# Large GpSimd instructions written as two halves each, and the new tokens' scores as plain fp32 matmuls, in a two-layer decoder step

## The chip, the core and the metric

The kernel runs on one NeuronCore of a Trainium2 chip. The metric is the device time of one execution in microseconds (us). The engines are called by the profile's names: PE (TensorE matmuls), PEld (its weight loads), DVE (VectorE), ACT (ScalarE), POOL (GpSimd) and SP (SyncE, which issues the DMAs). Each engine works through its own list of instructions in order.

## The reference, cut to what matters

Two layers run over 1024 prompt tokens and, in the same pass, over 64 new tokens: 8 sequences of 8 tokens, each with its own cache of old keys and values. Each layer projects every token to nine parts, and runs a gated branch and an attention branch with three dilation groups of 8 heads.

```python
u, v, z_a, q, k, val, z_b, g_a, g_b = split_projection(jnp.dot(h, w_in))
vn = layer_norm(jax.nn.gelu(v), gm_ln_g, gm_ln_b)
y_a = jax.nn.gelu(u) * gm_spatial(vn) * jax.nn.silu(z_a)      # gated branch
...
# new tokens, group g (window win, dilation dil: (128,1), (512,4), (2048,16)):
k_all = jnp.concatenate([buf[:, :, 0], k[:, :, g]], axis=1)   # cached keys, then the new ones
kg = jnp.take(k_all, idx, axis=1)
s = jnp.einsum('bthd,btjhd->bhtj', q, kg) * (HEAD_DIM ** -0.5)
p = jnp.exp(s - logsumexp(s)); o = jnp.einsum('bhtj,btjhd->bthd', p, vg)
```

## The kernel before, in words

All matrices are fp32. For the projections each operand is split in two fp32r parts, a high part (an ACT copy, L243) and the rest (a subtraction, L249, or L247 where POOL and DVE take half each); a product is then three matmuls, hi·hi, hi·lo and lo·hi (L741; L1382 behind the attention). `split` does this for weights (`whi`, `wlo`, 128x1024, subtraction on POOL) and for activations and cached rows (`chl`, `vhl`, `pt`, 128x512 or less, subtraction on DVE).

A layer is 80 jobs of one weight tile each (val, q and k; z_b, g_a, v, g_b, z_a, u). A job is three pieces, one for each token block (384, 384 and 320 columns): `piece` issues 24 matmuls on PE. Three times in a piece it calls `tick`, which moves the work beside the projections: the prompt's attention, the cached scores and values, and a queue of generators that each go on to their next `yield` when their turn comes. So the order of work on every engine is that in which the program writes it; what a `yield` more or less does is put the next instructions some eight matmuls of PE later or earlier. `pause(n)` is n yields; `idle(n)` first runs the urgent generators, then n yields.

Beside the projections run:

- `cache_step`, the cached keys and values of the two dilated groups: POOL multiplies a loaded key tile by the queries (L377, L381, tiles `kq`), DVE adds up (L386); POOL multiplies a value tile by the probabilities (L430, tiles `vq`), DVE adds up (L415, L416).
- `sample`, the rest of the new tokens: four k units (`weights(rg)`, two sequences each) and four v units (`outputs(rg)`). In a k unit, each sequence's queries are copied by ACT in six pieces into a zeroed tile `qb`, DVE subtracts the copies for the low part (L1218), and PE multiplies them by the 128 cached keys of group 0 (L1228, keys split as `chl`) and by the new keys (L1236); DVE puts both halves together in `rows` (L1242). L1264 ff. are the softmax. In a v unit, L1315 and L1316 multiply probabilities by split values (`chl`).
- `gmlp`, the gated branch: for each block of 128 tokens `stats` (transposes on PE, L1099; statistics on DVE), the block before's `spatial` (plain fp32 matmuls, L1132), two yields, then `normalise` (DVE, L1113). `ev_u` of the first u job needs all of it: `drain` goes on turning the generators until `gm_done`.
- `ada`, the modulation of the next layer (L602, L579), the rest of which is drained at the end of layer 0.

The prompt's attention uses `kz` (zeroed key tiles written by ACT, L240) and L870 for its scores.

Of the kernel before, what the change touches and what calls it, by code (L numbers as in the profile page):

```python
# [24 lines left out]
FT = mybir.dt.float32  # L25
# [7 lines left out]
NB = 8  # L33
# [146 lines left out]
class Builder:  # L180
# [166 lines left out]
    def scores(self, l, g, pr):  # L347
# [57 lines left out]
    def values(self, l, rg, pv):  # L405
# [101 lines left out]
    def setup(self):  # L507
# [28 lines left out]
        self.s_d = [[d([8, NB, NT, 128], f"sd{l}{g}") for g in (1, 2)] for l in range(L)]  # L536
        self.vn_d = [d([3, SMP, 512], f"vnd{l}") for l in range(L)]
# [517 lines left out]
    def gmlp(self, l):  # L1055
# [84 lines left out]
        for n in (8, 0, 1, 2, 3, 4, 5, 6, 7):  # L1140
# [3 lines left out]
            yield from self.pause(2)  # L1144
# [27 lines left out]
    def sample(self, l):  # L1172
        nc, a, ident = self.nc, self.a, self.pk("ident")
        whole = self.apool.tile([128, 6144], FR, name=self.nm("qb"), tag="act")
        big = whole[:, 0:768]
        pt = whole[:, 768:1536].rearrange("p (a b) -> p a b", b=128)
        qs, kn = [whole[:, o:o + 768].bitcast(FT).rearrange("p (a b) -> p a b", b=SMP) for o in (1536, 2304)]
        vw = whole[0:24, 3072:4096].rearrange("p (a b) -> p a b", a=2)
        sel2 = whole[:, 4096:4160]
        knh = whole[:, 4160:4352].rearrange("p (a b c) -> p a b c", a=2, b=12)  # L1180
        for t, d in ((qs, self.qs_d[l]), (kn, self.kn_d[l])):
            self.load(t, d.rearrange("c p t -> p c t"))
        t = self.half(name="sel2")[:, 0:64]
        self.load(t, a["pack"][:, NPACK:NPACK + 64])
        nc.gpsimd.memset(whole[:, 0:768].bitcast(FT), 0.0)
        nc.vector.memset(whole[:, 768:1536].bitcast(FT), 0.0)
        pstep = list(big.ap[0])[0]

        def diag(off, ap, h2):
            v = big[64 * h2:64 * h2 + 64]  # L1190
            return bass.AP(tensor=v.tensor, offset=v.offset + off, ap=[[pstep, 64]] + ap)
# [3 lines left out]
        for x, rg in units:  # L1195
            for b in (2 * rg, 2 * rg + 1):
                if x == "v":
                    seq += [a["vc1"][l, b, i] for i in range(2)]
                seq.append(a[x + "c0"][l, b])
# [6 lines left out]
        yield from self.idle(2)  # L1206
        pn = {}

        def weights(rg):
            rows = self.slot([128, 1024], name="rows")[:, 0:408]  # L1210
            for b2 in range(2):
                b = 2 * rg + b2
                cols = slice(8 * b, 8 * b + 8)
                for h2 in range(2):
                    for o, ap, src in self.q_places(qs, slice(64 * h2, 64 * h2 + 64), cols, h2):
                        hi, lo = diag(o, ap, h2), diag(o + 32, ap, h2)
                        self.copy(hi, src)
                        nc.vector.tensor_tensor(lo, src, hi.bitcast(FT), op=OP.subtract)  # L1218
                self.split(knh[:, 0], knh[:, 1], kn[:, :, cols])
                yield from self.idle(2)  # L1220
                s = [self.ps("s") for _ in range(2)]
                hi, lo = next(st)
                for kt in range(4):
                    first, last = kt % 2 == 0, kt % 2 == 1
                    c = slice(kt * 128, kt * 128 + 128)
                    mm = [(64, hi), (32, lo)]
                    for m, t in (mm[::-1] if last else mm):
                        nc.tensor.matmul(s[kt // 2][0:m, 0:128], big[:, kt * 64:kt * 64 + m], t[:, c],  # L1228
                                         start=first and m == 64, stop=last and m == 64)
                yield  # L1230
                for g in range(3):
                    for kt in range(4):
                        base = g * 256 + kt * 64
                        mm = [(64, 0), (32, 1)]
                        for m, e in (mm[::-1] if kt % 2 else mm):
                            nc.tensor.matmul(s[kt // 2][0:m, 128 + 8 * g:136 + 8 * g], big[:, base:base + m],  # L1236
                                             knh[:, e, g * 4 + kt, :], start=kt % 2 == 0 and m == 64,
                                             stop=kt % 2 == 1 and m == 64)
                for qd in range(2):
                    t = self.half(name="slo")[0:32, 0:152]  # L1240
                    self.copy(t, s[qd][32:64, 0:152])
                    nc.vector.tensor_tensor(rows[64 * b2 + 32 * qd:64 * b2 + 32 * qd + 32, 128:280], s[qd][0:32, 0:152], t,  # L1242
                                            op=OP.add)
                yield
# [465 lines left out]
```

## Time and profile before

| | |
|---|---|
| median of 3 runs | 3123.28 us (3117.01 to 3130.36) |
| the profiled execution | 3131.33 us, of which the span is 3129.5 us |
| PE busy | 3010.8 us |
| DVE, ACT, POOL busy | 1687.0, 1231.3, 1357.9 us |

The span runs from the first instruction to the last; what lies around it is 1.8 us. The profiled execution is 8 us longer than the median.

### The profile page before, as it was taken

The numbers are of one execution on the slowest core, as the hardware profiler recorded it, in microseconds if no ns is written. First come the engines' busy times: TensorE is split into PE (matmuls) and PEld (weight loads), VectorE is DVE, ScalarE is ACT, GpSimd is POOL, SyncE is SP. The second block draws the span as 40 slices with busy tenths as digits, with TensorE's granted clock in tenths as the row PEclk, the third lists the DMA queues.
The fourth block names the chain that finished last, engine by engine and source line by source line (L and its number), as shares of the span: only waits on it lengthen the run. The fifth ranks groups of instructions, "written<-read, shape, count | busy, mean of one in ns | idle before, by whom it ended". The sixth has DMA issues, their size and how long they took to land.

```text
span 3129.5 us, 51144 instructions
## 1 busy us (share of the span) xinstructions
PE 3010.8 (96%) x19136; PEld 2865.4 (92%) x19136; DVE 1687.0 (54%) x3583; ACT 1231.3 (39%) x3089; POOL 1357.9 (43%) x959
## 2 busy tenths in 40 slices
PE   6999999999998999999999999999999999999998
PEld 4999899999988998879989999999999889989998
DVE  7445546462265756466773545454513657553666
ACT  5454444444233133343444444444432331322432
POOL 4666556462143322123446755656612432222333
PEclk8999999999999999999999999999999999999999
DMA  6335353444353335466644364435343542434665
GB/s 223 113 103 119 98 101 120 95 121 84 112 180 113 122 108 167 157 236 227 211 153 134 86 142 81 119 106 114 106 81 119 171 130 95 138 102 149 223 211 172
DMA packets 262288, 425.92 MB, mean 136 GB/s; under 512 B 116140, under 2 KB 169144, under 8 KB 262040
## 3 DMA queue, kind: packets, MB, share of 16 engines
q1 hardware_dynamic: 262040, 422.65, 45.4%
q8 instruction: 151, 2.47, 0.3%
q14 instruction: 97, 0.79, 0.1%
HBM read 349.96 MB, written 72.61 MB: 135 GB/s over the span
## 4 chain that ended last, share of the span: by engine, by line
PE 82%; DVE 8%; DMA 4%; issue 3%; ACT 2%; POOL 1%; SPq 0%; DVEq 0%; ACTq 0%; POOLq 0%
PE pspj L741 53%; PE pspj L1382 14%; PE pss L870 4%; PE pso L916 3%; PE pspt L895 2%; PE psmi L602 1%; DMA kq<-in_kc_dram 1%; DVE qb L1218 1%; DMA craw<-in_wada_dram 1%; DVE chl L249 1%; PE psmi L998 1%; DMA wraw<-in_win_dram 1%; ACT whi L243 1%; PE pss L1236 1%; PE pspt L1132 1%
## 5 line engine op out<-in xcount | busy, mean ns | idle before, releaser
L741 PE MATMUL pspj<-act,whi 128*128 128x384 f32 (+1 forms) x7680 | 1967.0, 339 | 6.5 <-DVE act L674 3.5
L741 PEld LDWEIGHTS pspj<-act,whi 128*128 128x128 f32 x7680 | 1352.7, 190 | 42.4 <-issue 7.4
L741 PE MATMUL pspj<-act,wlo 128*128 128x384 f32 (+1 forms) x3840 | 1264.3, 329 | 2.3 <-POOL wlo L247 2.3
L249 POOL TENSOR_TENSOR wlo<-wraw,whi 128x1024 fp32r<-128x1024 f32 x154 | 371.4, 2411 | 970.5 <-ACT whi L243 766.5
L741 PEld LDWEIGHTS pspj<-act,wlo 128*128 128x128 f32 x3840 | 729.0, 190 | 3.4 <-POOL wlo L247 3.4
L1382 PE MATMUL pspj<-act,whi 128*128 128x384 f32 (+1 forms) x1536 | 373.4, 326 | 0.5 <-ACT act L243 0.4
L243 ACT ACTIVATE whi<-wraw 128x1024 fp32r<-128x1024 f32 x280 | 293.9, 1051 | 112.0 <-DMA wraw<-in_wgm_dram 48.1
L247 POOL TENSOR_TENSOR wlo<-wraw,whi 128x512 fp32r<-128x512 f32 x126 | 192.3, 1531 | 328.4 <-ACT whi L243 268.7
L882 ACT ACTIVATE ssb<-ssb,ast 128x128 f32<-128x128 f32 (+1 forms) x384 | 170.2, 444 | 394.2 <-DVE ast L878 394.1
L878 DVE CUSTOM_DVE_ANT_0 ssb<-pss,pack 128x128 f32<-128x128 f32 (+1 forms) x384 | 119.4, 348 | 318.1 <-PE pss L870 316.5
L1382 PEld LDWEIGHTS pspj<-act,whi 128*128 128x128 f32 x1536 | 270.0, 188 | 1.0 <-ACT act L243 0.7
L1382 PE MATMUL pspj<-act,wlo 128*128 128x384 f32 (+1 forms) x768 | 250.2, 326 | 0.0
L1010 ACT ACTIVATE th<-pspj 128x384 f32<-128x384 f32 x168 | 79.2, 471 | 428.6 <-PE pspj L741 396.5
L787 POOL TENSOR_TENSOR r<-r,sin 128x384 f32<-128x384 f32 x144 | 139.0, 965 | 141.4 <-DVE r L786 121.4
L249 DVE TENSOR_TENSOR chl<-craw,chl 128x512 fp32r<-128x512 f32 x182 | 147.2, 840 | 86.7 <-ACT chl L243 86.2
L377 POOL TENSOR_TENSOR kq<-kq,qb 128x1024 f32<-128x1024 f32 x64 | 153.5, 2404 | 63.1 <-DMA kq<-in_kc_dram 45.9
L381 POOL TENSOR_TENSOR kq<-kq,qb 128x512 f32<-128x512 f32 x128 | 167.6, 1314 | 19.8 <-DMA kq<-in_kc_dram 9.2
L386 DVE TENSOR_REDUCE sc<-kq 128x16 f32<-128x1024 f32 x128 | 155.7, 1216 | 21.2 <-POOL kq L377 20.7
L870 PE MATMUL pss<-kz,q 128*128 128x256 f32 x560 | 155.4, 385 | 10.6 <-ACT kz L240 10.6
L430 POOL TENSOR_TENSOR vq<-vq,pv 128x1024 f32<-128x1024 f32 x64 | 132.3, 2081 | 50.0 <-DMA vq<-in_vc_dram 20.6
L1382 PEld LDWEIGHTS pspj<-act,wlo 128*128 128x128 f32 x768 | 144.2, 188 | 0.0
L247 DVE TENSOR_TENSOR wlo<-wraw,whi 128x512 fp32r<-128x512 f32 x126 | 109.3, 868 | 40.0 <-ACT whi L243 36.5
(211 smaller groups left out, 3676.2 us busy)
## 6 DMA issues: line engine op xcount, KB each, us to landing
wraw<-in_win_dram SPq DMA_DIRECT2D x160, 512.0 KB
kq<-in_kc_dram SPq DMA_DIRECT2D x64, 512.0 KB
vq<-in_vc_dram SPq DMA_DIRECT2D x64, 512.0 KB
craw<-in_wada_dram SPq DMA_DIRECT2D x48, 512.0 KB
wraw<-in_wgm_dram SPq DMA_DIRECT2D x48, 512.0 KB
wraw<-in_wo_dram SPq DMA_DIRECT2D x48, 512.0 KB
kq<-in_kc_dram SPq DMA_DIRECT2D x64, 256.0 KB
craw<-in_vc_dram SPq DMA_DIRECT2D x32, 512.0 KB
```

The costliest lines, as they stand in the source:

```text
L243: self.nc.scalar.activation(hi, src, AF.Copy)
L247: e.tensor_tensor(lo[:, c], src[:, c], hi[:, c].bitcast(FT), op=OP.subtract)
L249: (eng or self.nc.vector).tensor_tensor(lo, src, hi.bitcast(FT), op=OP.subtract)
L377: nc.gpsimd.tensor_tensor(v, v, x, op=OP.mult)
L381: nc.gpsimd.tensor_tensor(v[:, f], v[:, 1], x[f], op=OP.mult)
L386: nc.vector.tensor_reduce(sc[:, :, i].rearrange("p h j -> p j h"), ts.pop(i)[0].rearrange("p a (j h d) -> p (a j) h d", h=2, d=64), axis=A ...
L430: nc.gpsimd.tensor_tensor(v, v, p.unsqueeze(3).to_broadcast([128, 2, 8, 64]), op=OP.mult)
L741: nc.tensor.matmul(ps[:, :w], a[:, k, :], h[:, b, k, :w], start=(n == 0), stop=(n == 23))
L787: nc.gpsimd.tensor_tensor(t2, t2, self.sin[:, s], op=OP.mult)
L870: nc.tensor.matmul(s[:, 256 * j:256 * j + 256], u["q"][:, 128 * b:128 * b + 128], self.kz[:, (b - n + j) % 4].rearrange("p h c -> p (h c)" ...
L882: nc.scalar.activation(x[:, h, :w], x[:, h, :w], AF.Exp, bias=st[:, h * 8 + b:h * 8 + b + 1], scale=-1.0, accum_out=st[:, 16 + h * 8 + b:1 ...
L1382: self.nc.tensor.matmul(ps[:, :w], ws[a][:, k, :], hs[b][k][:, :w], start=(n == 0), stop=(n == 3 * nk - 1))
```

## The change

GpSimd's subtractions of 128x1024 (L249) and 128x512 with an engine named, its key products of 128x1024 (L377) and its value products (L430) are each written as two instructions on half the columns: 154 + 64 + 64 + 10 instructions become twice as many. The second half of L247 and the 128x512 key products (L381) stay.

In `sample` the new tokens' queries are loaded once into a zeroed block-diagonal tile `qd` (unsplit fp32). The scores against the new keys are done ahead of the units, 12 matmuls of 128x64 in each layer, and go through DRAM (`n_d`) into `rows` by two more loads in each unit. The scores against the cached keys are 8 fp32 matmuls of 128x128 in each unit with `kz` (idle then, zeroed, written by ACT) as the stationary operand; the keys are loaded at the unit's start into `kraw`, where before they came split out of a stream that ran ahead. The stream now holds values alone. `idle` in `weights` becomes `pause`, with one `hurry` at its start. In `gmlp` the wait ahead of `normalise` is three yields. On PE, 128 matmuls of L1228 and 384 of L1236 go, and 64 + 24 fp32 matmuls come; on DVE, 96 instructions of L1218, 32 subtractions of splits and 32 of L1242 go.

```diff
+        elif eng:
+            m = src.shape[-1] // 2
+            for c in (slice(m), slice(m, None)):
+                eng.tensor_tensor(lo[:, c], src[:, c], hi[:, c].bitcast(FT), op=OP.subtract)
         else:
-            (eng or self.nc.vector).tensor_tensor(lo, src, hi.bitcast(FT), op=OP.subtract)
+            self.nc.vector.tensor_tensor(lo, src, hi.bitcast(FT), op=OP.subtract)
...
-                nc.gpsimd.tensor_tensor(v, v, x, op=OP.mult)
+                for c in (slice(0, 4), slice(4, 8)):
+                    nc.gpsimd.tensor_tensor(v[:, c], v[:, c], x[:, c], op=OP.mult)
...
-            p = pv[i // 4].rearrange("p (h j) -> p j h", h=8)[:, 2 * (i % 4):2 * (i % 4) + 2]
-            v = ts[i].rearrange("p j (h d) -> p j h d", h=8)
-            nc.gpsimd.tensor_tensor(v, v, p.unsqueeze(3).to_broadcast([128, 2, 8, 64]), op=OP.mult)
+            for e in range(2):
+                p = pv[i // 4].rearrange("p (h j) -> p j h", h=8)[:, 2 * (i % 4) + e]
+                v = ts[i][:, e].rearrange("p (h d) -> p h d", h=8)
+                nc.gpsimd.tensor_tensor(v, v, p.unsqueeze(2).to_broadcast([128, 8, 64]), op=OP.mult)
...
-            yield from self.pause(2)
+            yield from self.pause(3)
...
+        qd = whole[:, 1536:3072].bitcast(FT).rearrange("p (a b) -> p a b", b=2 * SMP)
+        kn = whole[:, 4160:4928].bitcast(FT).rearrange("p (a b) -> p a b", b=SMP)
...
+        raws = {}
+
+        def keys_in(rg):
+            raws[rg] = self.slot([128, 2, 512], name="kraw")
+            for b2 in range(2):
+                self.load(raws[rg][:, b2], a["kc0"][l, 2 * rg + b2])
...
+        for b in range(NB):
+            seq += [a["vc1"][l, b, i] for i in range(2)]
+            seq.append(a["vc0"][l, b])
...
+        t = self.slot([128, 4, 192], name="sn")
+        for g0, n in ((0, 2), (2, 1)):
+            ps = self.ps("s")
+            for c in range(4 * n):
+                nc.tensor.matmul(ps[:, 64 * c:64 * c + 64], qd[:, 4 * g0 + c], kn[:, 4 * g0 + c], start=True, stop=True)
+            for g in range(n):
+                self.copy(t.rearrange("p k (b g t) -> p (k b) g t", b=8, g=3)[:, :, g0 + g],
+                          ps[:, 256 * g:256 * g + 256].rearrange("p (k t) -> p k t", t=8))
+            yield
+        self.store(self.n_d[l].rearrange("k p x -> p k x"), t)
...
         def weights(rg):
+            yield from self.hurry()
             rows = self.slot([128, 1024], name="rows")[:, 0:408]
+            keys_in(rg)
+            for h2 in range(2):
...
+            yield from self.pause(4)
+            k = raws.pop(rg)
+            s = self.ps("s")
             for b2 in range(2):
-                b = 2 * rg + b2
-                cols = slice(8 * b, 8 * b + 8)
-                for h2 in range(2):
-                    for o, ap, src in self.q_places(qs, slice(64 * h2, 64 * h2 + 64), cols, h2):
-                        hi, lo = diag(o, ap, h2), diag(o + 32, ap, h2)
-                        self.copy(hi, src)
-                        nc.vector.tensor_tensor(lo, src, hi.bitcast(FT), op=OP.subtract)
-                self.split(knh[:, 0], knh[:, 1], kn[:, :, cols])
-                yield from self.idle(2)
...
+                    i = 4 * b2 + kt
+                    nc.tensor.matmul(s[:, 0:128], kz[:, 128 * i:128 * i + 128], k[:, b2, 128 * kt:128 * kt + 128],
+                                     start=i == 0, stop=i == 7)
...
+            self.copy(rows[:, 128:256], s[:, 0:128])
+            del k
```

On POOL, in the stretch where values and weights alternate (`vq` the value tiles, `wlo` the low parts of weights), before:

```order
L430 TENSOR_TENSOR vq_9382<-vq_9382,pv_9047 128x1024
L249 TENSOR_TENSOR wlo_9450<-wraw_9316,whi_9449 128x1024
L430 TENSOR_TENSOR vq_9427<-vq_9427,pv_9047 128x1024
L430 TENSOR_TENSOR vq_9477<-vq_9477,pv_9047 128x1024
L430 TENSOR_TENSOR vq_9532<-vq_9532,pv_9047 128x1024
L249 TENSOR_TENSOR wlo_9590<-wraw_9453,whi_9589 128x1024
```

After the change:

```order
L436 TENSOR_TENSOR vq_9740<-vq_9740,pv_9294 128x512 x2
L251 TENSOR_TENSOR wlo_9794<-wraw_9672,whi_9793 128x512 x2
L436 TENSOR_TENSOR vq_9782<-vq_9782,pv_9295 128x512 x2
L436 TENSOR_TENSOR vq_9826<-vq_9826,pv_9295 128x512 x2
L436 TENSOR_TENSOR vq_9863<-vq_9863,pv_9295 128x512 x2
L251 TENSOR_TENSOR wlo_9912<-wraw_9798,whi_9911 128x512 x2
L436 TENSOR_TENSOR vq_9901<-vq_9901,pv_9295 128x512 x2
```

Each instruction stands twice in its place, with half the columns, and nothing comes between the halves.

On DVE, in a k unit of layer 0 (`chl` split cached rows, `qb` the split queries, `rows` the scores), before:

```order
L249 TENSOR_TENSOR chl_8667<-craw_8627,chl_8667 128x512
L1218 TENSOR_TENSOR qb_8582<-qb_8582 64x2x2x8 x6
L249 TENSOR_TENSOR qb_8582<-qb_8582 128x96
L249 TENSOR_TENSOR chl_8732<-craw_8670,chl_8732 128x512
L1242 TENSOR_TENSOR rows_8697<-pss_8730,slo_8779 32x152
L1242 TENSOR_TENSOR rows_8697<-pss_8731,slo_8782 32x152
L1218 TENSOR_TENSOR qb_8582<-qb_8582 64x2x2x8 x6
```

None of these stands there afterwards. What fills `kz` and `rows` then is on ACT, here in a unit of layer 1 (`sn` the new scores, `th` and `whi` the projections' work):

```order
L240 ACTIVATE sn_24175<-pss_24196 128x32x8
L1017 ACTIVATE th_24209<-pspj_24165 128x384
L240 ACTIVATE kz<-qb_24059 64x8x8 x2
L1017 ACTIVATE th_24244<-pspj_24217 128x320
L243 ACTIVATE whi_24280<-wraw_24160 128x1024
L1017 ACTIVATE th_24288<-pspj_24246 128x384
L240 ACTIVATE rows_24211<-pss_24256 128x128
```

On PE at the first u job of layer 0, where `drain` runs (`vn` and `wm` the gated branch's, `pss` the scores), before:

```order
L741 MATMUL pspj_11405<-act_162,whi_11260 128x384 x2
L741 MATMUL pspj_11405<-act_162,wlo_11261 128x384
L1132 MATMUL pspt_11439<-wm_10785,vn_11415 128x128 x4
L1132 MATMUL pso_11440<-wm_10785,vn_11415 128x128 x4
L1228 MATMUL pss_11476<-chl_10494,qb_8582 64x128
L1228 MATMUL pss_11476<-chl_10494,qb_8582 32x128 x2
L1228 MATMUL pss_11476<-chl_10494,qb_8582 64x128
L1228 MATMUL pss_11477<-chl_10494,qb_8582 64x128
L1228 MATMUL pss_11477<-chl_10494,qb_8582 32x128 x2
L1228 MATMUL pss_11477<-chl_10494,qb_8582 64x128
L741 MATMUL pspj_11491<-act_163,whi_11260 128x384 x2
```

After the change the last two token blocks stand closer, with 15 matmuls of L748 (which was L741) between their products (L1139, which was L1132), the last of them here:

```order
L748 MATMUL pspj_11216<-act_164,wlo_11106 128x384
L748 MATMUL pspj_11216<-act_164,whi_11105 128x384 x2
L748 MATMUL pspj_11216<-act_164,wlo_11106 128x384
L1139 MATMUL pspt_11286<-wm_10572,vn_11283 128x128 x4
L1139 MATMUL pso_11287<-wm_10572,vn_11283 128x128 x4
L748 MATMUL pspj_11314<-act_165,whi_11105 128x384 x2
L748 MATMUL pspj_11314<-act_165,wlo_11106 128x384
```

and the key products (L1245) follow 18 matmuls later, with no split in front of them:

```order
L748 MATMUL pspj_11314<-act_165,whi_11105 128x384 x2
L748 MATMUL pspj_11314<-act_165,wlo_11106 128x384
L1245 MATMUL pss_11333<-kraw_11305,kz 128x128 x4
L748 MATMUL pspj_11314<-act_165,whi_11105 128x384 x2
L748 MATMUL pspj_11314<-act_165,wlo_11106 128x384
L748 MATMUL pspj_11314<-act_165,whi_11105 128x384 x2
L748 MATMUL pspj_11314<-act_165,wlo_11106 128x384
L1245 MATMUL pss_11333<-kraw_11305,kz 128x128 x4
```

The keys' loads are issued 17 matmuls ahead of them here; in the other units of a layer it is 39, 51 and 35.

## Rows read from the trace of the kernel before

**Rows 1.** The page's busy times and shares of the span, by engine (part 1).

```profile
PE 3010.8 (96%) x19136; PEld 2865.4 (92%) x19136; DVE 1687.0 (54%) x3583; ACT 1231.3 (39%) x3089; POOL 1357.9 (43%) x959
```

**Rows 2.** The page's chain that ended last, by engine (part 4).

```profile
PE 82%; DVE 8%; DMA 4%; issue 3%; ACT 2%; POOL 1%; SPq 0%; DVEq 0%; ACTq 0%; POOLq 0%
```

**Rows 3.** PE's waits: what waited, for whom: us in total, times, longest.

```profile
PE pss L1228 <- DVE qb L1218: 20.3, 6, 5.3
PE pspt L1315 <- DVE chl L249: 14.8, 16, 2.8
PE pss L870 <- ACT kz L240: 10.6, 7, 3.0
```

**Rows 4.** DVE in order of time: start, us, instruction, count [idle before].

```profile
288.07 1.86 DVE L969 TENSOR_TENSOR cmx<-cst 128x16 f32<-128x16 f32 x1
289.96 2.30 DVE L970 TENSOR_TENSOR cmx<-cmx,cst 128x16 f32<-128x16 f32 x1
```

**Rows 5.** POOL in order of time, the same stretch.

```profile
287.49 2.40 POOL L377 TENSOR_TENSOR kq<-kq,qb 128x1024 f32<-128x1024 f32 x1
289.84 2.40 POOL L249 TENSOR_TENSOR wlo<-wraw,whi 128x1024 fp32r<-128x1024 f32 x1
```

**Rows 6.** PE's matmul that waited at the end of it.

```profile
294.63 0.70 PE L870 MATMUL pss<-kz,q 128*128 128x256 f32 x2 [2.99 <-ACT kz L240]
```

**Rows 7.** Stretches behind waits of L1228: busy by engine, PEclk, DMA share.

```profile
949.80:957.60 7.80, 7.80 (x49) 7.70 (x50) 5.56 (x11) 2.22 (x5) 0.00 (x0) 0.50 0.20 69
...
2505.20:2514.10 8.90, 8.90 (x54) 8.80 (x55) 6.53 (x13) 2.21 (x5) 0.00 (x0) 0.50 0.28 79
sum 27.60, PE 27.59 PEld 27.25 DVE 17.43 ACT 5.50 POOL 0.00; mean PE 6.90 PEld 6.81 DVE 4.36 ACT 1.37 POOL 0.00
```

**Rows 8.** PE in order of time, a k unit whose matmuls didn't wait.

```profile
827.00 0.51 PE L741 MATMUL pspj<-act,whi 128*128 128x384 f32 x2
827.35 0.33 PE L741 MATMUL pspj<-act,wlo 128*128 128x384 f32 x1
827.52 0.64 PE L1228 MATMUL pss<-chl,qb 128*64 128x128 f32 x8
827.99 0.51 PE L741 MATMUL pspj<-act,whi 128*128 128x320 f32 x2
...
829.35 1.19 PE L1236 MATMUL pss<-qb 128*64 128x8 f32 x24
830.40 0.40 PE L741 MATMUL pspj<-act,whi 128*128 128x320 f32 x1
```

**Rows 9.** PE in order of time, plain fp32 products of the gated branch.

```profile
1063.88 1.06 PE L1132 MATMUL pspt<-wm,vn 128*128 128x128 f32 x8
1064.77 0.39 PE L1132 MATMUL pso<-wm,vn 128*128 128x128 f32 x2
```

**Rows 10.** POOL's groups by shape: count, busy us, mean ns, idle before.

```profile
L249 POOL TENSOR_TENSOR wlo<-wraw,whi 128x1024 fp32r<-128x1024 f32 x154 | 371.4, 2411 | 970.5 <-ACT whi L243 766.5 <-issue 117.4 <-DVE chl L249 35.4
...
L381 POOL TENSOR_TENSOR kq<-kq,qb 128x512 f32<-128x512 f32 x128 | 167.6, 1314 | 19.8 <-DMA kq<-in_kc_dram 9.2 <-PE pspj L741 4.1 <-DMA vnd<-vnew 1.6
L377 POOL TENSOR_TENSOR kq<-kq,qb 128x1024 f32<-128x1024 f32 x64 | 153.5, 2404 | 63.1 <-DMA kq<-in_kc_dram 45.9 <-DMA wraw<-in_win_dram 17.2
```

**Rows 11.** SyncE's DMA issues in order of time, loads of cached keys.

```profile
433.56 0.62 SPq L252 DMA_DIRECT2D kq<-in_kc_dram  x1
```

**Rows 12.** POOL's wait for those keys.

```profile
441.38 2.40 POOL L377 TENSOR_TENSOR kq<-kq,qb 128x1024 f32<-128x1024 f32 x1 [7.84 <-DMA kq<-in_kc_dram]
```

**Rows 13.** PE: products of the gated branch's last two token blocks, layer 0.

```profile
1104.51 1.06 PE L1132 MATMUL pso<-wm,vn 128*128 128x128 f32 x8
...
1110.46 1.05 PE L1132 MATMUL pspt<-wm,vn 128*128 128x128 f32 x8
```

**Rows 14.** DVE's normalisation of the last block.

```profile
1107.48 1.52 DVE L1113 TENSOR_SCALAR vn<-pss,mv 128x512 f32<-128x512 f32 x2
```

**Rows 15.** PE in the drain at layer 0's end, start of a turn.

```profile
1358.64 1.05 PE L579 MATMUL psmi<-pack,arow 18*128 18x10 f32 x8 [0.68 <-ACT arow L240]
```

More of the change, by code (lines that the diff above doesn't have):

```diff
@@ L536, in setup @@
         self.s_d = [[d([8, NB, NT, 128], f"sd{l}{g}") for g in (1, 2)] for l in range(L)]
+        self.n_d = [d([4, 128, 192], f"nd{l}") for l in range(L)]
         self.vn_d = [d([3, SMP, 512], f"vnd{l}") for l in range(L)]
@@ L1174, in sample @@
         whole = self.apool.tile([128, 6144], FR, name=self.nm("qb"), tag="act")
[L1175 removed]
         pt = whole[:, 768:1536].rearrange("p (a b) -> p a b", b=128)
[L1177 removed]
+        qd = whole[:, 1536:3072].bitcast(FT).rearrange("p (a b) -> p a b", b=2 * SMP)
+        kn = whole[:, 4160:4928].bitcast(FT).rearrange("p (a b) -> p a b", b=SMP)
+        kz = self.kz.rearrange("p a b c -> p (a b c)")
         vw = whole[0:24, 3072:4096].rearrange("p (a b) -> p a b", a=2)
         sel2 = whole[:, 4096:4160]
[L1180 to L1182 removed]
+        nc.gpsimd.memset(whole[:, 1536:3072].bitcast(FT), 0.0)
+        nc.gpsimd.memset(kz, 0.0)
+        self.load(kn, self.kn_d[l].rearrange("c p t -> p c t"))
+        for h2 in range(2):
+            r = slice(64 * h2, 64 * h2 + 64)
+            self.load(qd[r, :, r], self.qs_d[l][:, r].rearrange("c p t -> p c t"))
         t = self.half(name="sel2")[:, 0:64]
         self.load(t, a["pack"][:, NPACK:NPACK + 64])
[L1185 removed]
         nc.vector.memset(whole[:, 768:1536].bitcast(FT), 0.0)
[L1187 to L1191, printed above, removed]
+        raws = {}
[3 more added lines that the diff above has]
+                self.load(raws[rg][:, b2], a["kc0"][l, 2 * rg + b2])
         units = (("k", 0), ("k", 1), ("v", 0), ("k", 2), ("v", 1), ("k", 3), ("v", 2), ("v", 3))
         seq = []
[L1195 to L1199, printed above, removed]
+        for b in range(NB):
+            seq += [a["vc1"][l, b, i] for i in range(2)]
+            seq.append(a["vc0"][l, b])
         st = self.half_stream(seq, 1, 1)
@@ L1207, in sample @@
+        self.store(self.n_d[l].rearrange("k p x -> p k x"), t)
+        del t
         pn = {}
         def weights(rg):
+            yield from self.hurry()
             rows = self.slot([128, 1024], name="rows")[:, 0:408]
-            for b2 in range(2):
-                b = 2 * rg + b2
-                cols = slice(8 * b, 8 * b + 8)
-                for h2 in range(2):
-                    for o, ap, src in self.q_places(qs, slice(64 * h2, 64 * h2 + 64), cols, h2):
-                        hi, lo = diag(o, ap, h2), diag(o + 32, ap, h2)
-                        self.copy(hi, src)
-                        nc.vector.tensor_tensor(lo, src, hi.bitcast(FT), op=OP.subtract)
-                self.split(knh[:, 0], knh[:, 1], kn[:, :, cols])
-                yield from self.idle(2)
-                s = [self.ps("s") for _ in range(2)]
-                hi, lo = next(st)
-                for kt in range(4):
[L1224 to L1229, printed above, removed]
-                yield
[L1231 to L1244, printed above, removed]
-                yield from self.hurry()
@@ new lines, in weights @@
+            keys_in(rg)
+            for h2 in range(2):
+                v = kz[64 * h2:64 * h2 + 64]
+                pstep = list(v.ap[0])[0]
+                self.copy(bass.AP(tensor=v.tensor, offset=v.offset + 8 * h2, ap=[[pstep, 64], [576, 2], [144, 4], [1, 8]]),
+                          qd[64 * h2:64 * h2 + 64, 0:4, 64 * h2 + 16 * rg:64 * h2 + 16 * rg + 16]
+                          .rearrange("p k (b t) -> p b k t", t=8))
+            yield from self.pause(4)
+            k = raws.pop(rg)
@@ L1256, in scores_in @@
                                           ap=[[8192, 8], [128, 8], [1, 128]]))
+                    d = self.n_d[l]
+                    self.load(rows[64 * b2:64 * b2 + 64, 256:280],
+                              bass.AP(tensor=d.tensor, offset=d.offset + (8 * 192 + 24) * (2 * rg + b2),
+                                      ap=[[12288, 8], [192, 8], [1, 24]]))
                 went.append(True)
@@ L1261, in weights @@
                 yield
-            yield from self.idle(3)
+            yield from self.pause(3)
             mx = self.sm([128, 4], name="smx")
@@ L1269, in weights @@
             self.store(self.p_d[l][rg].rearrange("a b c -> (a b) c"), rows[:, 280:408])
-            yield from self.idle(4)
+            yield from self.pause(4)
             pp = self.ps("mi")
@@ L1338, in sample @@
             yield from (weights if x == "k" else outputs)(rg)
+        nc.gpsimd.memset(kz, 0.0)
         for c in range(4):
@@ L1342, in sample @@
         yield
-    def q_places(self, qs, pr, cols, h2):
-        out = []
-        for g in range(3):
-            src = qs[pr, 4 * g:4 * g + 4, cols].rearrange("p (a b) t -> p a b t", b=2)
-            out.append((256 * g + 8 * h2, [[128, 2], [80, 2], [1, 8]], src))
-        return out
     def p_places(self, pt, pn, b2):
```

## The prediction

> **What bounds the kernel now.** I read the page's busy times first: PE works through 3010.8 of 3129.5 us, POOL through 1357.9, DVE through 1687.0 [rows 1]. The chain that ended last says the same: 82% of it is PE, 8% DVE, 4% DMA, 1% POOL [rows 2]. So a change here is worth what it takes out of PE's list, what it takes out of PE's waits, and what it gives back of PE's clock. PE is idle for 3129.5 - 3010.8 = 118.7 us, and I read its waits next. The longest entry is L1228, the new tokens' scores, for DVE's subtractions L1218: 20.3 us in six waits. Then come L1315 (value products, for splits on DVE) with 14.8 and L870 (for ACT's `kz`) with 10.6 [rows 3].
>
> Why DVE and ACT are late is seen in one stretch, read on three engines. Two DVE instructions of 16 elements took 1.86 and 2.30 us, each until 289.9 and 292.3 [rows 4], and that is when a POOL instruction of 2.40 us beside each was over [rows 5]; what follows on DVE and ACT came late, and PE's matmul waited 2.99 us [rows 6]. So a DVE instruction that reads two tiles of SBUF stands still until the POOL instruction that runs beside it has ended.
>
> The waits have a second price. Behind four of the six L1228 waits are stretches, 27.60 us in all, in which the granted clock is about 0.50, the 1.2 GHz level instead of 2.4, with PE busy throughout (27.59 us) and just out of its wait; the first and the last of them show 0.50 [rows 7].
>
> **The change, term by term.** All of it is worked out for the profiled execution, 3131.33 us, and then moved to the median of the runs, 3123.28, which is 8 us less.
>
> *The waits of L1228.* The subtractions go, and nothing on DVE replaces them: the stationary operand `kz` is two plain ACT copies, issued four turns ahead of the matmuls, and ACT is 39% busy [rows 1]. All 20.3 us go: **-20.3** [rows 3].
>
> *The clock behind them.* At half speed a stretch loses half of itself: 27.6 x 0.5 = 13.8 us; two of the four show a little over 0.50, so I take 13.5. Without the wait ahead of it I expect the clock to stay: **-13.5** [rows 7].
>
> *PE's own work.* Eight L1228 matmuls hold PE from 827.52 to 827.99, 0.47 us, and 24 of L1236 from 829.35 to 830.40, 1.05 us [rows 8]; there are 16 such sequences, so 16 x 1.52 = 24.3 us go. What comes is plain fp32, which the records show as two entries for one matmul; four such matmuls of 128x128 (eight entries) hold PE from 1063.88 to 1064.77, 0.89 us [rows 9]. Sixteen groups of four make 14.2 us, and 24 matmuls of 128x64, priced from above by the same row, 24 x 0.22 = 5.3. Together 19.5: **-4.8**. The key products themselves become dearer, 0.89 for 0.47; the gain is all in L1236.
>
> *Halves on POOL.* A product of 128x1024 takes 2.40 us, one of 128x512 1.31 [rows 10], so two halves are 0.22 us longer than the whole: 292 x 0.22 = 64 us more on POOL, which is idle for 3129.5 - 1357.9 = 1772 us. If the 1% of the chain that is POOL, some 31 us, grew by 2.63/2.40 with nothing to hide it, that would be 3 us. I book none of it: POOL's largest group stands idle 766.5 us until ACT's copies come [rows 10], and that is its cover.
> What the halves can give: a DVE instruction stands still for the rest of a half instead of the rest of a whole, at most 2.40 - 1.31 = 1.1 us less each time. At L870's wait two such instructions stand in series, so 2.2 of its 2.99 us could go [rows 4 to 6]. Bounds over all: nothing, if what PE waited for is late for other reasons, and 14.8 + 10.6 = 25.4 us, if both entries go [rows 3]. The L1315 waits are 0.9 us on the mean, less than a half's gain, but loads can be behind some of them. I take the middle: **-12.7**. Half clock behind these waits I leave to the range.
> The Trainium skill bears on this in two pages. SBUF — State Buffer, section Who interferes with whom, says that a DVE instruction with two SBUF inputs contends with a GpSimd instruction that reads SBUF, and that whoever issues first has the shared port pair for the whole instruction; the rows of 1.86 and 2.30 us agree, and by that rule the stall ends with the half. Perfetto Trace Analysis, section Optimizing Scalar/DVE Operations, can be read against the change: larger operations improve throughput if the engine is saturated, while breaking up is for engines that are not saturated but cause bubbles elsewhere. By its first part the halves are a loss, which is a rival below; POOL's 43% fits its second.
>
> *New waits: the keys.* They were split out of a stream that ran ahead; now their load is issued at the unit's start, and PE has 39, 51, 35 and 17 matmuls before it needs them. At 0.17 us each (three from 827.00 to 827.52 [rows 8]) that is 6.6, 8.7, 6.0 and 2.9 us. From above: a load of cached keys of 512 KB, as much as a unit's two loads together, was issued at 433.56 [rows 11], and POOL, which waited 7.84 us for it, used it at 441.38 [rows 12], 7.8 us after the issue. That leaves 1.2, 0, 1.8 and 4.9, or 7.9 us in a layer, 15.8 in all; from below it is nothing, where the load lands within the lead. POOL's products of this size stood 45.9 us in all for 64 such loads [rows 10], so most landed in time, and I stand near the lower end: 2.5 us in all, on the short lead of 17. Behind the waiting product on PE is the projection itself, so such a wait is paid in full.
> *New waits: one more turn ahead of the normalisation.* For most blocks it moves work by a turn that nothing waits for, since projections lie between a block's statistics and its products. In the drain at the first u job the last block is short of them. Before, its rows were ready at 1107.48 + 1.52 = 1109.0 [rows 14] and used at 1110.46, while the products ahead started their second half at 1104.51 and ended some 0.9 later, near 1105.4 [rows 9, 13]. So the rows come 3.6 us after those products; afterwards 15 matmuls of PE lie between, 2.5 us, so PE waits 1.1 us in each layer, 2.2. Both together, with a little clock: **+5**.
> The two more loads into `rows` in a unit lie beside ACT and DVE work of the same unit, three turns ahead of its softmax, which the v units need only later; nothing, and if they were late the softmax would be, not PE.
>
> *The drain at layer 0's end* has one turn less. Its matmuls are done earlier instead, so only the turn's wait is saved, 0.68 us [rows 15]: **-0.7**.
>
> Sum: -20.3 - 13.5 - 4.8 - 12.7 + 5 - 0.7 = -47.0. From 3131.33 this gives 3084; from the median **3076 us**. The bounds of the terms (halves from 0 to -25.4, new waits from 2.2 to 18) put this case between 3052 and 3096.
>
> **The rivals.** A measurement of this kernel can tell about 0.5%, 15.6 us, from no change.
>
> *The halves give nothing, or cost.* PE's waits were late for loads and ACT's copies, and POOL's 3 us are paid: -47.0 + 12.7 + 3 = -31.3, **3092**. For it: the L1315 waits are sixteen short ones, without one cause that repeats. Against: rows 4 to 6. The saturation rule of the skill's trace page would lead here too. Chance 0.14.
>
> *The halves give more.* All 25.4 us go, and some 5 us of clock behind them, as behind L1228: -47.0 - 12.7 - 5 = -64.7, **3059**. Chance 0.06.
>
> *The score waits only move.* If `kz`'s copies stand behind other ACT work, or the clock falls at the same places for other reasons, the 20.3 + 13.5 stay: -13.2, **3110**. Against: ACT has four turns for two copies. Chance 0.08, of which 0.03 on the side that can be measured.
>
> *The keys land late in each unit: slower.* If SyncE's issue is held up, by a buffer not yet free or by loads in front, the lead is gone, and each of the eight units waits up to the 7.8 us of rows 12, followed by a half-clock stretch that loses some 4 us, as the first of rows 7: 8 x 11.8 = 94, less the 2.5 booked, **3168**. It decides from (47.0 + 2.5) / 8 = 6.2 us a unit, where no gain is left; from 8.1 us the kernel is slower by over 0.5%. For it: leads of 3 to 9 us against a load that took 7.8. Against: for three units of four the lead is about the load's time, and DMA is 4% of the chain. Chance 0.10, half of it near no change, half beyond.
>
> **How the numbers follow.** The forecast has 0.62, with 3052 to 3096 as its own range. The range that leaves out 2 in 10 runs from 3048 to 3108: it holds the forecast, both cases of the halves and the edge of the moved waits. Faster by over 0.5% (under 3107.7): 0.62 + 0.14 + 0.06 + 0.03 = 0.85; within: 0.05 + 0.05 = 0.10; slower: 0.05.
>
> **What would show it.** In the profile afterwards L1218, L1228 and L1236 are gone, and no entry of PE's waits for the key products (L1245) is over 3 us. The places of the four slow stretches have a clock near full. PE's busy time falls by some 18 us, since half-clock stretches count as busy (13.5 + 4.8). POOL's busy time is about 1420 us, its large instructions at 1.3 us. The entries of L1315 and L870 are about half. It would be wrong if PE waited for `kraw` in several units, if half-clock stretches came up at new places, or if L870 and L1315 kept their waits with the halves beside them.

## The result, and the profile after

The changed kernel takes 3078.68 us at the median of four runs (3075.79 to 3083.39), the kernel before beside it 3121.09. The ratio is 0.9856, with a 95% interval of 0.984 to 0.9872: 40 to 50 us less, where 47 were forecast. In a second comparison (`e9_after`, below) it was 0.9871 (0.9853 to 0.989).

The page's busy times, of the changed kernel (answers to [rows 1]):

```profile
PE 2984.9 (97%) x18800; PEld 2844.8 (92%) x18800; DVE 1595.0 (52%) x3423; ACT 1205.5 (39%) x2959; POOL 1425.9 (46%) x1255
```

The span is 3081.6 us, 47.9 less. PE's busy time fell by 25.9 us, its idle time from 118.7 to 96.7, by 22.0. POOL works 68 us more, as was worked out (64).

PE's waits, of the changed kernel (us in total, times, longest; [rows 3] before):

```profile
PE pso L1334 <- DVE oh L1330: 11.7, 7, 3.4
PE pspt L1323 <- DVE chl L253: 9.5, 11, 1.4
...
PE pss L877 <- ACT kz L240: 6.1, 6, 2.3
...
PE pspt L1139 <- DVE vn L1120: 1.7, 2, 0.9
```

No wait for the key products (L1245) stands among them. The splits' wait (L1323, before L1315) is 9.5 after 14.8, `kz`'s (L877, before L870) 6.1 after 10.6. A wait that was 4.8 us before, at the end of a value unit (L1334), is now the longest, with 11.7.

The stretch of [rows 4 to 6], as it is now. DVE in order of time:

```profile
288.82 0.75 DVE L976 TENSOR_TENSOR cmx<-cst 128x16 f32<-128x16 f32 x1
289.60 1.21 DVE L977 TENSOR_TENSOR cmx<-cmx,cst 128x16 f32<-128x16 f32 x1
```

POOL beside it, two halves in each row:

```profile
288.25 2.53 POOL L382 TENSOR_TENSOR kq<-kq,qb 128x512 f32<-128x512 f32 x2
290.74 2.52 POOL L251 TENSOR_TENSOR wlo<-wraw,whi 128x512 fp32r<-128x512 f32 x2
```

ACT's copy ahead of `kz`, and what it waited for:

```profile
293.29 0.38 ACT L243 ACTIVATE pt<-pspt 128x256 fp32r<-128x256 f32 x1 [0.91 <-POOL wlo L251]
```

PE's matmul that waited:

```profile
294.45 0.70 PE L877 MATMUL pss<-kz,q 128*128 128x256 f32 x2 [2.34 <-ACT kz L240]
```

The two DVE instructions take 1.96 us where they took 4.16: the 2.2 us less of the forecast, to the tenth. The first ends at 289.57 and the second at 290.81, each about when one of the two halves of L382 is over (some 289.5 and 290.78). PE's wait yet fell by only 0.65 us, from 2.99 to 2.34, and ACT's copy in front of it stood 0.91 us until POOL's second half of L251 was over at 293.26. A stall of DVE ends with the half. The copy does not read what L251 writes; that it waited for a buffer is inferred, and by that reading what needs the whole result, or its buffer, waits for both halves.

### The profile page after: what moved, and what is told of

Read it like the earlier page. It is cut to its first block, busy times and chain, and to the rows that moved or that the text cites. A ratio compares the mean times of both kernels' runs of the same rounds, so it can differ in the third digit from the quotient of the medians.

```text
span 3081.6 us, 50575 instructions
## 1 busy us (share of the span) xinstructions
PE 2984.9 (97%) x18800; PEld 2844.8 (92%) x18800; DVE 1595.0 (52%) x3423; ACT 1205.5 (39%) x2959; POOL 1425.9 (46%) x1255
## 4 chain that ended last, share of the span: by engine, by line
PE 83%; DVE 7%; DMA 4%; ACT 3%; issue 2%; POOL 1%; SPq 0%; DVEq 0%; ACTq 0%; POOLq 0%
PE pspj L748 54%; PE pspj L1384 13%; PE pss L877 4%; PE pso L923 3%; PE pspt L902 2%; PE psmi L609 1%; DVE vq L420 1%; PE psmi L1005 1%; DVE vq L421 1%; PE pspt L1323 1%; DMA craw<-in_wada_dram 1%; DMA wraw<-in_win_dram 1%; ACT whi L243 1%; PE psmi L845 1%; PE pspt L1139 0%
## 5 line engine op out<-in xcount | busy, mean ns | idle before, releaser
L748 PE MATMUL pspj<-act,whi 128*128 128x384 f32 (+1 forms) x7680 | 1956.2, 338 | 6.2 <-DVE act L681 3.2
L748 PEld LDWEIGHTS pspj<-act,whi 128*128 128x128 f32 x7680 | 1343.5, 189 | 41.6 <-issue 7.0
L748 PE MATMUL pspj<-act,wlo 128*128 128x384 f32 (+1 forms) x3840 | 1259.7, 328 | 2.5 <-POOL wlo L247 2.5
L251 POOL TENSOR_TENSOR wlo<-wraw,whi 128x512 fp32r<-128x512 f32 x308 | 398.0, 1313 | 886.6 <-ACT whi L243 616.9
L748 PEld LDWEIGHTS pspj<-act,wlo 128*128 128x128 f32 x3840 | 724.8, 189 | 3.6 <-POOL wlo L247 3.6
L247 POOL TENSOR_TENSOR wlo<-wraw,whi 128x512 fp32r<-128x512 f32 x126 | 192.9, 1536 | 331.3 <-ACT whi L243 281.8
L382 POOL TENSOR_TENSOR kq<-kq,qb 128x512 f32<-128x512 f32 x128 | 164.7, 1311 | 58.8 <-DMA kq<-in_kc_dram 51.4
L436 POOL TENSOR_TENSOR vq<-vq,pv 128x512 f32<-128x512 f32 x128 | 155.5, 1241 | 43.9 <-DMA vq<-in_vc_dram 12.9
L386 POOL TENSOR_TENSOR kq<-kq,qb 128x512 f32<-128x512 f32 x128 | 165.7, 1299 | 20.2 <-DMA kq<-in_kc_dram 8.7
L253 DVE TENSOR_TENSOR chl<-craw,chl 128x512 fp32r<-128x512 f32 x166 | 126.3, 789 | 77.6 <-ACT chl L243 77.1
L877 PE MATMUL pss<-kz,q 128*128 128x256 f32 x560 | 154.4, 383 | 6.1 <-ACT kz L240 6.1
L247 DVE TENSOR_TENSOR wlo<-wraw,whi 128x512 fp32r<-128x512 f32 x126 | 106.9, 849 | 46.5 <-ACT whi L243 42.0
```

What stands on the lines that cost most here:

```text
L251: eng.tensor_tensor(lo[:, c], src[:, c], hi[:, c].bitcast(FT), op=OP.subtract)
L382: nc.gpsimd.tensor_tensor(v[:, c], v[:, c], x[:, c], op=OP.mult)
L386: nc.gpsimd.tensor_tensor(v[:, f], v[:, 1], x[f], op=OP.mult)
L436: nc.gpsimd.tensor_tensor(v, v, p.unsqueeze(2).to_broadcast([128, 8, 64]), op=OP.mult)
L748: nc.tensor.matmul(ps[:, :w], a[:, k, :], h[:, b, k, :w], start=(n == 0), stop=(n == 23))
L877: nc.tensor.matmul(s[:, 256 * j:256 * j + 256], u["q"][:, 128 * b:128 * b + 128], self.kz[:, (b - n + j) % 4].rearrange("p h c -> p (h c)" ...
```

## The experiments

All ratios are to the kernel before, in runs on the same chip.

**Halves and scores apart.** `e1_scores` is the changed kernel with these instructions whole again (and so for L377 and L430):

```diff
-        elif eng:
-            m = src.shape[-1] // 2
-            for c in (slice(m), slice(m, None)):
-                eng.tensor_tensor(lo[:, c], src[:, c], hi[:, c].bitcast(FT), op=OP.subtract)
         else:
-            self.nc.vector.tensor_tensor(lo, src, hi.bitcast(FT), op=OP.subtract)
+            (eng or self.nc.vector).tensor_tensor(lo, src, hi.bitcast(FT), op=OP.subtract)
```

> The changed kernel with GpSimd's large instructions whole again: the scores' part and the step in the gated branch alone. By the prediction's terms the scores' part is worth 20.3 + 13.5 + 4.8 us and the halves 12.7, so this should stand some 34 us below the kernel before and 13 us above the changed kernel (ratio 0.989), and the waits for the value splits and for kz should be back near 14.8 and 10.6 us. Rival: the halves give nothing, then it is as fast as the changed kernel (ratio 0.9856). Second rival: the halves do most of it, then it is within 10 us of the kernel before (0.997).

Measured: 0.9929 (0.9908 to 0.995), some 22 us less than before, where 34 were expected. The page and PE's waits of this run:

```profile
PE 2997.0 (96%) x18800; PEld 2852.7 (92%) x18800; DVE 1628.8 (52%) x3423; ACT 1205.8 (39%) x2959; POOL 1363.1 (44%) x963
```

```profile
PE pspt L1317 <- DVE chl L249: 14.3, 15, 1.9
PE pss L871 <- ACT kz L240: 9.9, 6, 3.0
...
PE pso L1328 <- DVE oh L1324: 8.4, 4, 4.1
...
PE pspt L1306 <- DVE qb L1302: 4.4, 4, 1.4
```

L1228's 20.3 us are gone, but PE's idle time is 3106.6 - 2997.0 = 109.6 us, only 9.1 less than before. The value units' first product (L1306), which did not wait before, has 4.4 us, and their last (L1328) 8.4 for 4.8: together 8.0 of the 11.2 us that did not come back. One place of it, on DVE and on PE, and the granted clock behind it (last column but two):

```profile
994.77 2.30 DVE L416 TENSOR_TENSOR vq<-vq 128x512 f32<-128x512 f32 x1
997.00 0.68 DVE L1322 TENSOR_TENSOR om<-pspt,pack 128x512 f32<-128x512 f32 x1
997.71 1.01 DVE L1324 TENSOR_REDUCE oh<-om 128x64 f32<-128x512 f32 x1
```

```profile
998.78 0.47 PE L1328 MATMUL pso<-pack,oh 128*64 128x64 f32 x2 [4.06 <-DVE oh L1324]
```

```profile
998.90:1004.00 5.10, 5.10 (x17) 4.98 (x18) 3.05 (x6) 1.77 (x3) 0.92 (x1) 0.50 0.06 8
```

In the kernel before, the same product (the fourth sequence of layer 0) waited 0.58 us. Now PE comes there earlier, and DVE has just taken 2.30 us for an instruction that takes 0.69 at 986.10, beside a whole product of cached values on POOL (994.06 to 996.53). So I read it as a wait that moved from one unit's product to another's, and its half clock with it; that is read from this place and the two entries, not tried. This run also has the third step ahead of the normalisation, which alone makes the kernel before slower (`e10_pause3`, below). Its waits for the normalised rows are 2.1 us here, so they do not account for the missing 12 us, but the scores' part was not run without the step.

`e2_halves` is the kernel before with the halves alone (the same lines the other way round).

> The kernel before with the halves alone. If a DVE instruction stands still only until the POOL instruction beside it has ended, the waits of L1228 fall from 20.3 us to about 10, the clock behind them comes back in part (4 of 13.5 us), and the value and kz waits lose what they lost in the changed kernel: some 25 us below the kernel before (ratio 0.992). If DVE waits for both halves, or POOL's longer work gives it back, no change (1.000).

Measured: 0.9936 (0.9915 to 0.9957), 20 us less. PE's waits:

```profile
PE pspt L1321 <- DVE chl L253: 10.8, 16, 2.4
PE pss L1234 <- DVE qb L1224: 9.5, 6, 2.0
...
PE pss L876 <- ACT kz L240: 6.2, 6, 2.4
```

L1234, which was L1228, waits 9.5 us in six waits for 20.3: half, as a stall that ends with the piece gives it. Drops of 0.0064 and 0.0071 alone make 0.0135, and both edits together gave 0.0144 and 0.0129. So the two parts add up.

**Which halves.** `e5_weights` keeps the halves of the weights' subtractions and `e6_cache` those of the cached keys' and values' products, the others whole.

> The changed kernel with halves for the weights' subtractions alone; the products with cached keys and values are whole again. All halves together took it from 0.9929 to 0.9856. If each part gives in proportion to POOL's time in it (371 of 657 us), this stands at 0.989. Rival: PE's waits lie in the value units, where the cached values' products run back to back, so the weights' halves give nothing (0.993). Second rival: a DVE instruction most often meets the weights, and this alone gives nearly all (0.986).

> The other way round: halves for the products with cached keys and values alone, the weights whole. In proportion 0.990; by the first rival of the run with the weights' halves alone 0.986, by the second 0.993. If both parts alone give little and together 0.0073, they act on the same waits in series.

Measured: 0.991 (0.9895 to 0.9925) and 0.9885 (0.9867 to 0.9902). Against 0.9929 without any, the cache's halves give 0.0044, clear of the intervals, and the weights' 0.0019, which is not; together 0.0063 of the 0.0058 to 0.0073 that both give. The cache's products have the smaller share of POOL's time. That speaks against a gain in proportion to POOL's time, but only just: of the two ratios that proportion asks for, 0.989 lies a little outside the first interval and 0.990 inside the second.

**Quarters.** `e4_quarters`:

```diff
-            m = src.shape[-1] // 2
-            for c in (slice(m), slice(m, None)):
+            m = src.shape[-1] // 4
+            for c in (slice(i * m, i * m + m) for i in range(4)):
```

> The changed kernel with quarters in place of halves (128x256 each). If the stall ends with the piece, the waits that are left for the value splits, kz and the end of a value unit (27 us together) shrink by a quarter to a half, 7 to 13 us faster than the changed kernel (ratio 0.982). If each piece's fixed cost, about 0.2 us, decides, POOL works some 120 us more and its results come later: the same as the changed kernel or slower (0.986 to 0.990).

Measured: 0.9851 (0.9828 to 0.9874), the same as with halves. The page:

```profile
PE 2982.9 (97%) x18800; PEld 2841.6 (92%) x18800; DVE 1570.6 (51%) x3423; ACT 1207.0 (39%) x2959; POOL 1535.4 (50%) x1839
```

DVE is busy 24 us less than in the changed kernel, as it would be if its stalls went on shrinking, and POOL 109 us more. PE's waits:

```profile
PE pspt L1324 <- DVE chl L253: 8.1, 14, 1.1
PE pspj L610 <- POOL chl L251: 7.9, 7, 2.1
PE pso L1335 <- DVE oh L1331: 7.7, 7, 2.7
```

The three entries that the expectation names fell from 27.3 to 21.2 us (`kz` from 6.1 to 5.4), but the wait for POOL's own splits (L610, which is L609 in the changed kernel) rose from 4.0 to 7.9. PE's idle time is 94.5 us for 96.7, and the time does not show it.

**The keys' lead.** `e7_keys_late` issues the keys' loads right ahead of their products:

```diff
-            keys_in(rg)
             for h2 in range(2):
...
             yield from self.pause(4)
+            keys_in(rg)
             k = raws.pop(rg)
```

> The changed kernel with the cached keys' loads issued right ahead of their products, four turns later, so that each of the eight units waits for the whole load. This prices a PE wait with what follows it. By the prediction's rival 5 to 8 us of wait and some 4 us of half clock behind each: 72 to 94 us above the changed kernel (ratio 1.009 to 1.016). If the clock does not fall behind such a wait, the waits alone: 40 to 62 us (0.998 to 1.006). If SyncE's queue runs ahead of PE so that the load is still early, less than 20 us (below 0.992).

Measured: 0.9888 (0.9869 to 0.9906), some 5 to 10 us above the changed kernel, which is not clear of the intervals: the third case of the expectation. PE's entry for the keys, then the second unit's issue on SyncE and its product on PE:

```profile
PE pss L1245 <- DMA kraw<-in_kc_dram: 2.9, 3, 1.2
```

```profile
859.40 1.22 SPq L256 DMA_DIRECT2D kraw<-in_kc_dram  x2
```

```profile
862.72 1.02 PE L1245 MATMUL pss<-kraw,kz 128*128 128x128 f32 x7 [1.06 <-DMA kraw<-in_kc_dram]
```

SyncE reached the first issue 3.3 us before PE's product began, though the program has them side by side, and of these 3.3 us PE waited 1.06. Three units of eight waited, 1.2 us at most. So the rival in which the keys are late in each unit is out, even without a lead in the program. What else the 5 to 10 us are made of, if they are more than noise, was not found.

**A turn more or less.** `e3_pause2` takes the third step out of the changed kernel again, `e11_pause4` adds a fourth, `e10_pause3` puts the third alone into the kernel before, and `e9_after` is the changed kernel itself:

```diff
             if before:
                 spatial(*before)
-            yield from self.pause(3)
+            yield from self.pause(2)    # e3; 4 in e11; e10: 2 becomes 3
```

> The changed kernel with two steps ahead of the normalisation, as before. By the prediction the third step costs only the wait in the drain of the first u job (1.7 us in the changed kernel's trace), so this is 2 us faster or the same (ratio to before 0.985). Rival: the third step is what keeps DVE from standing behind the normalisation, then this is slower than the changed kernel by the stall of 16 blocks, up to 0.5 us each, 8 us (0.988).

> The changed kernel itself, so that the three beside it are compared on one chip: ratio 0.9856 again (0.984 to 0.987).

> The kernel before with the third step ahead of the normalisation as its only edit. By the prediction's term it costs the wait in the drain of the first u job, 2.2 us: no change (1.000 to 1.001). From the changed kernel with two steps (0.9877 against 0.9856) the step is worth 6 us there; if it gives that by itself, by keeping PE from standing behind the gated branch's constants and the value units, the ratio is 0.998. If its worth there came only from how the pieces of the changed kernel fall together, anything between 0.996 and 1.004 can come out.

> The changed kernel with a fourth step. The gated branch then ends eight turns later, so more of it runs in the drain of the first u job, where PE has nothing else: as with the later end of a value unit (0.9919), waits of 2 to 3 us for the normalised rows in each layer and half clock behind them, 8 to 15 us more: 0.988 to 0.991. Rival: the step's worth grows with it, another 6 us less: 0.984.

Measured: 0.9877 (0.9856 to 0.9898), 0.9871 (0.9853 to 0.989), 1.0057 (1.004 to 1.0075) and 0.9917 (0.9902 to 0.9931). The step alone makes the kernel before 18 us slower; in the changed kernel two steps or three can't be told apart, and four cost 14. PE in the drain of the first u job of `e10_pause3`, in order of time:

```profile
1109.13 1.81 PE L1099 MATMUL pss<-pack,sp 128*128 128x128 f32 x8 [2.47 <-DVE vn L1113]
...
1115.62 1.63 PE L1132 MATMUL pspt<-wm,vn 128*128 128x128 f32 x8 [1.98 <-DVE vn L1113]
...
1120.78 0.66 PE L1228 MATMUL pss<-chl,qb 128*64 128x128 f32 x8 [1.82 <-DVE qb L1218]
```

Three waits stand where the kernel before has one of 1.97 us (L1228, part of its 20.3). They do not explain the 18 us: over this whole execution PE is idle 119.6 us for 118.7, because other entries are shorter, and the execution is the fastest of its six (3135.11 us, with a median of 3143.06). So that the step costs 18 us is measured, and where most of it lies stays open. PE's waits in `e11_pause4`:

```profile
PE pss L1106 <- DVE vn L1120: 6.4, 4, 2.3
...
PE pspt L1139 <- DVE vn L1120: 3.9, 2, 2.0
```

It is the same place: the end of the gated branch, with no projections left to lie between. Here PE is idle 104.1 us, 7.0 more than in `e9_after`.

`e8_fin` and `e12_fin1` have three yields and one instead of two ahead of the product that ends a value unit's sequence.

> The changed kernel with one more turn ahead of the product that ends a value unit's sequence (L1334), whose waits for DVE are 11.7 us in the changed kernel. If such a wait is only too short a distance, some 10 us and the clock behind it go: ratio 0.982. If the waits move with the work, to the value splits or the next unit's first product, as the scores' waits did, no change (0.985 to 0.987).

> The changed kernel with one turn less ahead of the product that ends a value unit's sequence (L1334). One turn more cost 20 us (0.9919). If the distance in itself decides, one turn less makes DVE late at each of the 16 sequences, a turn is 1.4 us of PE, so up to 20 us more: 0.988 to 0.992. If it is the end of the gated branch that decides, which comes earlier with fewer turns, the waits in the drain go (1.7 us) and it is the same or faster: 0.983 to 0.986.

Measured: 0.9919 (0.9904 to 0.9935) and 0.9918 (0.9904 to 0.9932), 15 to 20 us slower both ways. PE's waits, of the one and the other:

```profile
PE pspt L1323 <- DVE chl L253: 17.0, 14, 2.2
...
PE pss L1106 <- DVE vn L1120: 6.7, 4, 2.7
...
PE pspt L1139 <- DVE vn L1120: 4.2, 2, 2.2
```

```profile
PE pso L1333 <- DVE oh L1330: 12.7, 8, 2.5
...
PE pspj L748 <- ACT th L1017: 8.8, 2, 4.8
```

With a turn more, L1334's 11.7 us shrink to 3.7, but the splits' wait grows from 9.5 to 17.0, and the gated branch ends late again (6.7 and 4.2). With a turn less that wait stays (12.7), and new ones come at the projections for ACT (8.8).

## Why the prediction was right, and where it was not

The time lies 3 us from the forecast, and the range held it. That the sum came so near is luck: two of its terms missed on opposite sides, the scores' part by 12 us and the halves by 5 to 10. The range itself does not follow from the bounds given for it: with the halves from 0 to -25.4 and the new waits from 2.2 to 18 the sum runs from -62.5 to -21.3, which from the median is 3061 to 3102 and not 3052 to 3096. The measured time lies in both.

**The waits of L1228 (-20.3) and the clock behind them (-13.5): the waits went, the gain did not stay whole.** The step "All 20.3 us go" is true of the entry and not of PE's idle time. With its other terms the scores' part was forecast at 34.3 us (-20.3 - 13.5 - 4.8 + 5 - 0.7) and measured at 22 (16 to 29 by the interval). The rival "the score waits only move" was right for about a third: `e1_scores` shows waits at L1306 and L1328, with half clock behind. I had said that nothing on DVE replaces the subtractions; the stalls beside POOL that had held DVE up were still there, as at 994.77 above, for the next consumer.

**PE's own work (-4.8): right in kind, if anything a little more.** In `e1_scores` PE is busy 13.8 us less. The mean granted clock of the run went from 0.981 to 0.984, which is 3129.5 x 0.019 - 3106.6 x 0.016 = 9.8 us of the span (to some 3 us, by the clock's last digit); 4.0 are left. PE's list in the changed kernel gives it more directly:

```profile
830.36 1.05 PE L1245 MATMUL pss<-kraw,kz 128*128 128x128 f32 x8
831.16 0.60 PE L748 MATMUL pspj<-act,whi 128*128 128x384 f32 x2
```

Four key products hold PE for 0.80 us where 0.89 was taken. Sixteen such groups make 12.8 us; eight of the 128x64 matmuls hold it from 819.97 to 821.68, so 24 make 5.1. With the 24.3 us that went this is 6.4 us less.

**The halves (-12.7): mis-sized.** They are worth 18 to 23 us (0.0058 to 0.0073 of the kernel before; 20 alone, in `e2_halves`). In PE's idle time the term holds: 109.6 us in `e1_scores`, 96.7 in the changed kernel, 12.9 less. The rest is in PE's busy time, which I left to the range. How much of that is clock stays open: the changed kernel's two profiled executions differ in it. The second, `e9_after`:

```profile
PE 2989.2 (97%) x18800; PEld 2849.4 (92%) x18800; DVE 1589.6 (52%) x3423; ACT 1206.2 (39%) x2959; POOL 1425.1 (46%) x1255
```

Its idle time is the same 97 us, but PE is busy 4.3 us longer, with a mean clock of 0.984 for 0.987, and `e1_scores` has 0.984 too.
The way the halves act is shown: half the wait at L1234 in `e2_halves`, and DVE's two instructions above. The Trainium skill (SBUF — State Buffer, section Who interferes with whom) says that a DVE instruction with two SBUF inputs contends with a GpSimd instruction that reads SBUF, and calls the shared port pair an exclusive lock; the rows agree, 1.86 and 2.30 us beside whole instructions and 0.75 and 1.21 beside halves. At the one wait that the prediction read in full, L870's of 2.99 us, DVE gave back the 2.2 us and PE only 0.65. The Trainium skill's other page in the prediction (Perfetto Trace Analysis, section Optimizing Scalar/DVE Operations) speaks of Scalar and DVE, and of larger operations on a saturated engine. GpSimd is busy 46% of the span here, and its 68 us more did not show in the time, nor did 109 more in quarters.

**What I did not foresee: L1334.** DVE, ahead of a wait of 3.37 us there, in the changed kernel:

```profile
1152.93 1.66 DVE L1173 TENSOR_TENSOR gu<-gu,zz 128x384 f32<-128x384 f32 x1 [1.65 <-ACT gu L1172]
1154.62 1.30 DVE L1175 TENSOR_TENSOR gu<-gu,sp 128x384 f32<-128x384 f32 x1
1155.85 1.55 DVE L253 TENSOR_TENSOR chl<-craw,chl 128x512 fp32r<-128x512 f32 x1
1157.32 1.55 DVE L420 TENSOR_TENSOR vq<-vq,vq 128x512 f32<-128x512 f32 x1
...
1160.97 1.02 DVE L1330 TENSOR_REDUCE oh<-om 128x64 f32<-128x512 f32 x1
```

POOL beside it:

```profile
1154.13 8.13 POOL L436 TENSOR_TENSOR vq<-vq,pv 128x512 f32<-128x512 f32 x6
```

PE's product:

```profile
1162.13 0.30 PE L1334 MATMUL pso<-pack,oh 128*64 128x64 f32 x2 [3.37 <-DVE oh L1330]
```

Six halves run back to back, right behind the two of a weight (L251, 1151.63 to 1154.17). Each of the five DVE instructions beside these eight that read two operands from SBUF (the fifth, L421, is not shown) takes 1.3 to 1.7 us; a split of 128x512 (L253) with POOL idle, at 1150.59, takes 0.69. One stall is shorter, but there are more of them in a row when the products bunch. This is read at one of the seven waits, and a version without the bunching was not tried.

**New waits (+5).** The keys: none, for 2.5. The bound of 7.8 us came from one load, with the DMA engines busy 98% of the time between its issue and its use; in `e7_keys_late` the second unit's keys were there 3.3 us after the first issue, at 89%. Why the one took longer stays open. The normalised rows in the drain: 1.7 us in two waits (L1139), for 2.2. Alone the same edit cost 18 us (`e10_pause3`). I put the difference down to the gated branch, which in the changed program starts two pieces earlier (4344 matmuls of the projections stand ahead of its first transposes, for 4392); that was not tried by itself.

**The drain at layer 0's end (-0.7)** was not tested by itself. Its entry of PE's waits (L586, before L579) has four waits for five, and 4.7 us for 4.9.

**The clock at the four places.** Over the new tokens' part of both layers, where the kernel before had the four stretches of [rows 7], the changed kernel's rows have the full granted clock (the last column but two):

```profile
820.00:1320.00 500.00, 485.83 (x2920) 453.27 (x2918) 255.72 (x476) 157.47 (x322) 168.68 (x139) 1.00 0.44 146
2370.00:2830.00 460.00, 446.99 (x2689) 426.62 (x2689) 229.24 (x433) 129.37 (x265) 166.37 (x137) 1.00 0.40 130
```

That holds for this execution alone. In `e9_after`, the same program, both rows have 0.99, and a half-clock stretch stands at a new place, which the prediction named as a sign of being wrong: behind the wait at L1334 shown above, here as long as there.

```profile
1164.88 0.45 PE L1334 MATMUL pso<-pack,oh 128*64 128x64 f32 x2 [3.38 <-DVE oh L1330]
```

The stretch behind it in `e9_after`, then the one behind the same wait in the first execution:

```profile
1165.00:1170.00 5.00, 5.00 (x19) 4.88 (x20) 4.12 (x10) 2.20 (x8) 0.01 (x1) 0.50 0.53 180
```

```profile
1162.50:1167.50 5.00, 5.00 (x32) 5.00 (x33) 4.12 (x12) 2.54 (x9) 0.00 (x0) 1.00 0.61 202
```

After the same wait of 3.4 us the clock is at 0.50 in one execution and at 1.00 in the other. So the term "the clock behind them" priced what may follow such a wait, not what must.

PE's busy time, which was to fall by 18 us, fell by 25.9; POOL's 1425.9 was forecast as 1420.

## What to carry to other kernels

A wait that is taken from an engine that is busy 96% of the time can come back in part at the next consumer of the same late engine: here the entry's 20.3 us went and PE's idle time fell by 9.1, and with the clock 22 us came of the 34 booked. So book the cause of the lateness (here POOL's long instructions), not the entry. Where the order of work is written in turns, price an edit that adds or drops a turn by its worst place, in two of the runs here the end of a branch that something drains; in this kernel four edits of one turn cost 14 to 20 us each, about as much as either half of the change gave, and a fifth (`e3_pause2`) nothing that could be told. And a total that comes out right says little of its terms: only the parts run alone showed that one of them was off by 12 us and another by 5 to 10.

## What the runs showed that I had not expected

Quarters of POOL's instructions are as good as halves, though POOL worked 1535 us for 1426. The clock behind one and the same wait fell in one execution and not in another. The same kernel's mean granted clock was 0.987 in one execution and 0.984 in another, 3083.39 and 3088.12 us, so the clock's part of a difference of ten us can't be read from one profile of each.
